# Three stacked blocks on one core: the dilated logarithm folded into a bias table, a mask added in pieces, one PSUM pool, and another order in the last expert

## The chip, the cores and the metric

The kernel runs on one core of a Trainium2 chip. The metric is the device time of one execution in microseconds; smaller is better. Engine names are those of the profile: PE is TensorE (PEld its weight loads), DVE is VectorE, ACT is ScalarE, POOL is GpSimd, SP is SyncE, which here issues nearly all loads.

## What is computed

Three blocks follow each other on x, 256 tokens by 1024 columns, float32.

```python
# first block: Fourier mixing and a gated convolution, then experts that choose their tokens
probs = softmax(h @ w_router + b_router)
vals, idx = top_k(probs.T, cap)                 # 16 experts, 32 tokens each
y = (silu(xe @ w_gate_e) * (xe @ w_up_e)) @ w_down_e * vals
x = rms_norm(x + gate_f * scatter_add(y, idx), g_final)
# second block: one wide projection, two kinds of attention, gates, an output projection
proj = rms_norm_2(x, norm_pre) @ w_in
# third block, two layers: four kinds of attention side by side, then a feed-forward part
o_a = neighborhood_attention(..., rpb)          # rpb as a bias, columns outside a window masked
o_b = diff_attention(..., t5_table[:, :4])      # bias by bucketed distance
o_c = dilated_attention(..., t5_table[:, 4:])   # three patterns (128,1), (512,4), (2048,16), merged
o_d = mla_attention(...)
x = x + concat(o_a, o_b, o_c, o_d) @ w_o
x = x + (silu(h @ w_gate) * (h @ w_up)) @ w_down
```

Three dilated softmaxes merged by their sums are one softmax in which a key counts as often as patterns reach it. The kernel therefore adds the logarithm of that count (-1e30 where it is zero) to the dilated heads' bias. The count depends on the distance of key and query alone.

## The kernel before

Projections of the first, second and third block split each float32 weight piece into a high part (a cast on ACT, L125) and the rest (a subtraction on DVE, L126), and multiply three times on PE: high by high (L173), high input by low weight (L174), low input by high weight (L175). Each projection of 512 columns uses two PSUM banks, one for each half of the tokens. The experts multiply float32 directly, four column groups of the array at a time (gate and up at L851, down at L901).

PSUM has eight banks. The class `Net` opens three pools: `mm` with five banks, `tr` with two (transposes), and `po` with one. Projections, scores, gathers and the experts' sums come from `mm`. The Fourier outputs, one accumulator of the first block's modulation, the router's logits, the experts' up product, and the outputs of all attention heads come from `po`.

The program is written down in one order, and the framework lays it out into the engines' queues: an instruction that is ready earlier by its estimate may go ahead of one that was written first. Each queue is then worked off in order. `tc.issue_after(ins)` queues the instructions of its block behind `ins` where they are on the same engine, with no wait; `N.queued()` does it behind the last matmul noted in `N.last_mm`. Loads are chained in written order (`Net.load`).

In `moe` (the experts) the 16 experts run one after the other: gate and up products, `hs` (L867, L868), transposes to `hT`, then down. The scaled sum `Y` (L903) goes through a matmul with the scatter matrix into four banks `acc` (L907) that stay for all experts. The last expert, whose down weights are packed by columns, makes its two halves of 512 columns one after the other, and calls `out(n)` after each. `out` adds `acc` to x (L813), transposes the new columns and scales and splits them to `hx` (L271, L284, L285), takes squares (L260), and multiplies x by a gain on POOL (L821). During this the first 512-column projection of the second block is begun: `next_load` fetches half of its weights (four k tiles) and splits them in place (`split_to`, two pieces of two k tiles), and `next_products` multiplies them (L173 to L175 with `wr` and `hx`; 24 matmuls a call). The order written is: down half 0, `out(0)`, `next_load`, four k tiles of down half 1, `next_products`, the other twelve, `out(1)` with the second `next_load` in it, `next_products`. The down weights of half 1 come as one load of 2 MB and two of 1 MB, behind the first load of the projection.

In `mixers` (attention of the third block) the four kinds of heads are generators that step once per piece of the running projections: first the latent heads (`latent`, then `heads`), then `differential`, the neighbourhood heads, the dilated heads. A head's scores (L1413) take a bank, `softmax` reads it (L1395 or L1399 on DVE, L1404 on ACT) and scales (L1420), transposes follow (L1426, L1428), then the output product (L1453). `na_bias` loads the neighbourhood bias `nb` and adds the column mask on POOL in one instruction of 128x2048 (L1366). `dil_bias` loads the dilated heads' part `t5b` of the table (L1352) and `c_dil` (L1372), the logarithms for all pairs, and adds them on POOL, four times 128x512 (L1374). The table itself is made once, in `bias_rows` at the end of the first block: eight rows (heads) by 512 distances, from a matmul with a one-hot matrix (L1307), copied to `t5sb` on DVE (L1309), written to memory by POOL's queue (L1310) and broadcast (L1311).

## Time and profile before

| | before |
|---|---|
| median of 3 runs | 2061.4 us (2057.15 to 2067.67) |
| the profiled execution | 2060.89 us, span 2059.1 us |
| PE busy | 1658.0 us (81%) |
| PE weight loads | 997.9 us (48%) |
| DVE busy | 810.1 us (39%) |
| ACT busy | 602.7 us (29%) |
| POOL busy | 171.9 us (8%) |
| moved by DMA | 616.24 MB, mean 299 GB/s |

The page cuts the span into 40 slices of 51.5 us and gives for each engine the busy share in tenths. Matmuls overlap, so PE's busy time says less than its idle time: in the timelines a row's bracket gives the time that the engine stood idle before it, and what ended that. A row whose count is over 1 covers several instructions in a row, from the start of the first to the end of the last. Matmuls of float32 have two records each.

### The profile page before, as it was taken

The numbers are of one execution on the slowest core, as the hardware profiler recorded it, in microseconds if no ns is written. First come the engines' busy times: TensorE is split into PE (matmuls) and PEld (weight loads), VectorE is DVE, ScalarE is ACT, GpSimd is POOL, SyncE is SP. The second block draws the span as 40 slices with busy tenths as digits, with TensorE's granted clock in tenths as the row PEclk, the third lists the DMA queues.
The fourth block names the chain that finished last, engine by engine and source line by source line (L and its number), as shares of the span: only waits on it lengthen the run. The fifth ranks groups of instructions, "written<-read, shape, count | busy, mean of one in ns | idle before, by whom it ended". The sixth has DMA issues, their size and how long they took to land.

```text
span 2059.1 us, 22375 instructions
## 1 busy us (share of the span) xinstructions
PE 1658.0 (81%) x8897; PEld 997.9 (48%) x8897; DVE 810.1 (39%) x1565; ACT 602.7 (29%) x1075; POOL 171.9 (8%) x135
## 2 busy tenths in 40 slices
PE   7999796665655565656555799999999999999998
PEld 4777631111111111111111387777768888768886
DVE  4788610000000000000000357786885555785554
ACT  4455410000000000000000245555554445555443
POOL 1652100000000000000000131102000000110000
PEclk9999898768788888887887999999999999999999
DMA  9988789999999999999999873446335556525552
GB/s 361 378 297 340 319 363 429 429 428 429 430 428 430 429 428 431 429 430 429 429 428 430 332 257 127 143 136 221 117 103 184 184 172 218 170 68 184 184 174 72
DMA packets 128441, 616.24 MB, mean 299 GB/s; under 512 B 8264, under 2 KB 17672, under 8 KB 101328
## 3 DMA queue, kind: packets, MB, share of 16 engines
q1 hardware_dynamic: 124336, 601.46, 74.1%
q0 software_dynamic: 3568, 12.75, 1.9%
q8 instruction: 70, 1.15, 0.2%
q10 hardware_dynamic: 432, 0.60, 0.1%
q14 instruction: 35, 0.29, 0.0%
HBM read 613.72 MB, written 4.24 MB: 300 GB/s over the span
## 4 chain that ended last, share of the span: by engine, by line
PE 47%; DMA 43%; DVE 6%; issue 2%; ACT 1%; SPq 1%; POOL 0%; POOLq 0%; ACTq 0%; DVEq 0%
DMA wr<-we_gate_dram 13%; DMA wr<-we_up_dram 13%; DMA wr<-we_down_dram 13%; PE pb L173 13%; PE pb L174 12%; PE pb L175 12%; DMA wr<-w_in_dram 2%; DVE wl L126 2%; PE pb L271 1%; DMA wr<-w_ada_dram 1%; PE pb L851 1%; PE pb L1413 1%; PE pb L901 1%; ACT sb L1404 1%; PE pb L793 1%
## 5 line engine op out<-in xcount | busy, mean ns | idle before, releaser
L126 DVE TENSOR_TENSOR wl<-wr,wh 128x1024 fp32r<-128x1024 f32 (+1 forms) x380 | 410.2, 1088 | 263.5 <-ACT wh L125 260.0
L851 PE MATMUL pb<-wr,XT 128*32 128x512 f32 x2048 | 319.4, 753 | 214.7 <-DMA wr<-we_up_dram 121.6
L125 ACT CAST wh<-wr 128x1024 fp32r<-128x1024 f32 (+1 forms) x380 | 339.9, 898 | 329.8 <-PE pb L175 302.3
L173 PE MATMUL pb<-wh,hx 128*128 128x512 f32 (+3 forms) x992 | 388.5, 392 | 3.4 <-ACT sb L1404 2.0
L174 PE MATMUL pb<-wl,hx 128*128 128x512 f32 (+3 forms) x992 | 376.6, 380 | 1.7 <-DVE wl L126 1.6
L175 PE MATMUL pb<-wh,hx 128*128 128x512 f32 (+3 forms) x992 | 377.2, 381 | 0.0
L851 PEld LDWEIGHTS pb<-wr,XT 128*32 128x32 f32 x2048 | 61.3, 124 | 454.5 <-DMA wr<-we_up_dram 198.4
L901 PE MATMUL pb<-wr,hT 128*32 128x512 f32 x1024 | 172.7, 803 | 103.0 <-DMA wr<-we_down_dram 96.4
L868 DVE TENSOR_TENSOR hs<-pb,hs 128x512 f32<-128x512 f32 x16 | 11.1, 691 | 554.9 <-PE pb L851 554.9
L173 PEld LDWEIGHTS pb<-wh,hx 128*128 128x128 f32 x992 | 187.2, 189 | 44.0 <-issue 5.8
L174 PEld LDWEIGHTS pb<-wl,hx 128*128 128x128 f32 x992 | 187.7, 189 | 36.5 <-DVE wl L126 4.5
L175 PEld LDWEIGHTS pb<-wh,hx 128*128 128x128 f32 x992 | 187.4, 189 | 35.4 <-issue 0.7
L867 ACT ACTIVATE hs<-pb 128x512 f32<-128x512 f32 x16 | 9.6, 598 | 535.3 <-PE pb L851 534.2
L901 PEld LDWEIGHTS pb<-wr,hT 128*32 128x32 f32 x1024 | 33.9, 129 | 221.0 <-DMA wr<-we_down_dram 143.2
L903 DVE TENSOR_TENSOR Y<-pb,gfr 128x512 f32<-128x512 f32 x15 | 10.4, 692 | 247.1 <-PE pb L901 247.1
L881 ACT COPY Sc<-pb 128x256 f32<-128x256 f32 x16 | 6.0, 373 | 310.3 <-PE pb L879 310.3
L821 POOL TENSOR_TENSOR x<-x,grow 128x512 f32<-128x512 f32 x4 | 5.6, 1420 | 890.5 <-ACT jk L260 890.5
L173 PE MATMUL pb<-wh,ah 128*128 128x512 f32 x176 | 69.9, 397 | 0.0
L174 PE MATMUL pb<-wl,ah 128*128 128x512 f32 x176 | 69.6, 395 | 0.0
L175 PE MATMUL pb<-wh,al 128*128 128x512 f32 x176 | 69.6, 395 | 0.0
L907 PE MATMUL acc<-Y,Sc 64*128 64x512 f32 (+1 forms) x128 | 40.7, 714 | 18.3 <-DVE Y L903 18.3
L404 POOL TENSOR_SCALAR wr<-wr,cs 128x768 f32<-128x768 f32 x14 | 40.3, 2878 | 31.3 <-DMA wr<-w_ada_dram 26.4
(504 smaller groups left out, 1727.4 us busy)
## 6 DMA issues: line engine op xcount, KB each, us to landing
wr<-we_gate_dram SPq DMA_DIRECT2D x64, 2048.0 KB, 38.9
wr<-we_up_dram SPq DMA_DIRECT2D x64, 2048.0 KB, 39.0
wr<-we_down_dram SPq DMA_DIRECT2D x63, 2048.0 KB, 38.9
wr<-w_in_dram SPq DMA_DIRECT2D x62, 1024.0 KB, 8.0
wr<-w_ada_dram SPq DMA_DIRECT2D x24, 1024.0 KB, 12.7
wr<-w_gate_dram SPq DMA_DIRECT2D x22, 1024.0 KB, 5.1
wr<-w_up_dram SPq DMA_DIRECT2D x22, 1024.0 KB, 5.0
wr<-w_down_dram SPq DMA_DIRECT2D x20, 1024.0 KB, 5.0
```

Of the source, the lines that this page charges most:

```text
L125: self.nc.scalar.copy(hi, src)
L126: self.nc.vector.tensor_tensor(lo, src, hi.bitcast(F32), ALU.subtract)
L173: nc.tensor.matmul(o, xh[:, kt, tok], hv[:, k, :], start=kt == first, stop=False)
L174: nc.tensor.matmul(o, xh[:, kt, tok], lv[:, k, :], start=False, stop=False)
L175: self.last_mm = nc.tensor.matmul(o, xl[:, kt, tok], hv[:, k, :], start=False, stop=kt == last).ins
L271: self.nc.tensor.transpose(pv[:, j, h * P:(h + 1) * P], src[:, h, (k + j) * P:(k + j + 1) * P], self.ident)
L404: nc.gpsimd.tensor_scalar(wp, wp, cs[:, k:k + 1], None, ALU.mult)
L793: nc.tensor.matmul(pg, part[:, h, k * P:(k + 1) * P], G[:, h, es].rearrange("p e c -> p (e c)"), start=(h == 0 and i == 0), stop=(h == 1 a ...
L851: N.last_mm = nc.tensor.matmul(pacc[32 * j:32 * j + 32, :], XT[:, k + kk, e, :], wt[:, kk, j * 512:(j + 1) * 512], start=(k + kk == 0), st ...
L901: nc.tensor.matmul(py[32 * q:32 * q + 32, :], hT[:, b, 32 * j:32 * j + 32], wt[:, i, n * 512 - c0:n * 512 - c0 + 512], start=first, stop=l ...
L907: nc.tensor.matmul(acc[n][h], Sc[r, h * P:(h + 1) * P], Y[r, :], start=(e == 0), stop=(e == NE - 1))
L1404: nc.scalar.activation(sb[:, c], (ps if bias is None else sb)[:, c], AF.Exp, bias=mm[:, h:h + 1], accum_out=sm[:, h:h + 1])
```

## The change

- `po` is gone; `mm` has six banks, and all that took a bank from `po` takes one from `mm`.
- Last expert: `next_load` becomes a generator. `out(n)` starts it in both halves, right after the sums into x: the load first, the split queued behind the last of these sums on DVE. The pieces that wait to be multiplied are single k tiles (four a load), and `next_products(n)` multiplies n of them, 6 matmuls each. The order written for half 1 is: eight k tiles of down, two pieces, the other eight k tiles, Y, one piece, L907, the sums into x, one piece, the transposes; the second load's four pieces come last. The down matmuls of half 1 and the pieces are queued on PE in this order.
- `na_bias` adds the mask in eight instructions of 128x256.
- `dil_bias` is gone: `c_dil` is now the logarithm by distance (512 values for the four dilated heads, zeros for the other four), and is added in `bias_rows` when the table is made.

```diff
-        self.mm, self.tr, self.po = ps("mm", 5), ps("tr", 2), ps("po", 1)
+        self.mm, self.tr = ps("mm", 6), ps("tr", 2)
...
             for h in range(2):
                 add = nc.vector.tensor_tensor(x[:, h, cc], acc[n][h], x[:, h, cc], ALU.add).ins
+            ahead = next_load()
+            next(ahead)
+            with tc.issue_after(add):
+                next(ahead, None)
             if n:
-                with tc.issue_after(add):
-                    next_load()
+                next_products(1)
             N.in2.columns(n)
...
         def next_load():
+
             at, raw = next(loads)
             t = N.slot(F32R, wide=True)
-            N.ahead += [(k, p, N.split_to(t[:, 2048 * i:2048 * i + 2048], p)) for i, (k, p) in enumerate(N.pieces(raw, at))]
-
-        def next_products():
+            yield
+            for i, (k, p) in enumerate(N.pieces(raw, at)):
+                hv, lv = N.split_to(t[:, 2048 * i:2048 * i + 2048], p)
+                N.ahead += [(k + j, p[:, j:j + 1], (hv[:, j:j + 1], lv[:, j:j + 1])) for j in range(p.shape[1])]
+
+        def next_products(n=4):
+
             N.ahead_ps = N.ahead_ps or [N.bank(N.mm), N.bank(N.mm)]
-            for k, piece, hl in N.ahead:
-                N.proj_piece(N.ahead_ps, N.in2.hi, N.in2.lo, k, piece, 512, hl=hl)
-            N.ahead = []
+            for k, piece, hl in N.ahead[:n]:
+                with N.queued():
+                    N.proj_piece(N.ahead_ps, N.in2.hi, N.in2.lo, k, piece, 512, hl=hl)
+            del N.ahead[:n]
 
         for e in range(NE):
-            psG, psU = N.bank(N.mm), N.bank(N.po)
+            psG, psU = N.bank(N.mm), N.bank(N.mm)
...
                 c0 = 512 * ns[0]
-                if c0:
-                    next_load()
                 py = N.bank(N.mm)
...
-                        if c0 and at + i == 4:
-                            next_products()
+                        if c0 and at + i == 8:
+                            next_products(2)
...
-                            nc.tensor.matmul(py[32 * q:32 * q + 32, :], hT[:, b, 32 * j:32 * j + 32], wt[:, i, n * 512 - c0:n * 512 - c0 + 512],
-                                             start=first, stop=last, tile_position=(0, 32 * q))
+                            with N.queued() if c0 else nullcontext():
+                                mm = nc.tensor.matmul(py[32 * q:32 * q + 32, :], hT[:, b, 32 * j:32 * j + 32],
+                                                      wt[:, i, n * 512 - c0:n * 512 - c0 + 512],
+                                                      start=first, stop=last, tile_position=(0, 32 * q))
+                            if c0:
+                                N.last_mm = mm.ins
                 nc.vector.tensor_tensor(Y, py, rt.gf if e < NE - 1 else rt.gf_last[:, ns[0], :], ALU.mult)
+                if c0:
+                    next_products(1)
...
-    nc.vector.tensor_copy(sb, pb[:8, :])
+    nc.gpsimd.dma_start(sb, a["c_dil"])
+    nc.vector.tensor_tensor(sb, pb[:8, :], sb, ALU.add)
...
-            nv = nb.rearrange("p h n (r c) -> p (h n r) c", c=64)
-            nc.gpsimd.tensor_tensor(nv, nv, nmask.unsqueeze(1).to_broadcast([P, 32, 64]), ALU.add)
+
+            for h in range(2):
+                for n in range(4):
+                    nv = nb[:, h, n, :].rearrange("p (r c) -> p r c", c=64)
+                    nc.gpsimd.tensor_tensor(nv, nv, nmask.unsqueeze(1).to_broadcast([P, 4, 64]), ALU.add)
             return nb
-
-        def dil_bias():
-            td = t5_bias(4, "t5b")
-            dm = N.m2.tile([P, 2, S], F32, tag="m2", name="dm")
-            nc.gpsimd.dma_start(dm, a["c_dil"].rearrange("p (h k) -> p h k", h=2))
-            for n in range(4):
-                nc.gpsimd.tensor_tensor(td[:, n], td[:, n], dm, ALU.add)
-            return td
...
-        td = dil_bias()
+        td = t5_bias(4, "t5b")
```

## Rows read from the trace of the kernel before

**Rows 1.** The page's forty slices: busy tenths of PE, DVE and the DMAs.
```profile
PE   7999796665655565656555799999999999999998
DVE  4788610000000000000000357786885555785554
DMA  9988789999999999999999873446335556525552
```

**Rows 2.** Busy time by stretch: stretch, length, PE, PEld, DVE, ACT, POOL, clock, DMA, GB/s.
```profile
600.00:1000.00 400.00, 231.64 (x1406) 51.86 (x1406) 18.10 (x35) 6.20 (x13) 0.00 (x0) 0.82 1.01 429
...
1200.00:1250.00 50.00, 49.80 (x389) 40.93 (x388) 25.30 (x54) 26.02 (x41) 3.41 (x3) 1.00 0.54 182
```

**Rows 3.** Timeline, last expert's first half: start, length, engine, line, operation, idle before.
```profile
1151.55 1.92 PE L901 MATMUL pb<-wr,hT 128*32 128x512 f32 x16 [1.19 <-DMA wr<-we_down_dram]
...
1154.38 1.99 ACT L125 CAST wr<-wr 128x1024 fp32r<-128x1024 f32 x2 [8.50 <-DMA wr<-w_in_dram]
1155.46 1.23 DVE L126 TENSOR_TENSOR wr<-wr 128x1024 fp32r<-128x1024 f32 x1 [9.53 <-ACT wr L125]
1156.61 0.68 DVE L903 TENSOR_TENSOR Y<-pb,gfl 128x512 f32<-128x512 f32 x1
...
1157.43 3.45 PE L907 MATMUL acc<-Y,Sc 128*128 128x512 f32 x4 [3.96 <-DVE Y L903]
...
1161.67 0.87 PE L271 MATMUL pb<-ident,x 128*128 128x128 f32 x6 [0.56 <-DVE x L813]
```

**Rows 4.** Timeline of PE, last expert's second half; the first of 24 products, then what follows.
```profile
1163.47 0.50 PE L173 MATMUL pb<-wr,hx 128*128 128x512 f32 x1
...
1169.14 2.78 PE L901 MATMUL pb<-wr,hT 128*32 128x512 f32 x24
...
1172.74 1.98 PE L907 MATMUL acc<-Y,Sc 128*128 128x512 f32 x4 [0.81 <-DVE Y L903]
...
1175.51 0.87 PE L271 MATMUL pb<-ident,x 128*128 128x128 f32 x6 [0.16 <-DVE x L813]
```

**Rows 5.** Timeline of PE: idle time in the Fourier part and in the mixer layers.
```profile
82.14 0.70 PE L520 MATMUL pb<-V,fc 128*128 128x256 f32 x2 [0.61 <-DVE f L126]
...
1449.69 0.70 PE L1413 MATMUL pb<-qkT 96*128 96x256 f32 x2 [1.88 <-ACT sb L1404]
...
1494.55 0.55 PE L1426 MATMUL pb<-ident,sb 128*128 128x128 f32 x3 [0.89 <-DVE sb L1420]
...
1772.60 0.50 PE L173 MATMUL pb<-wh,hx 128*128 128x512 f32 x1 [2.02 <-ACT sb L1404]
...
1776.38 0.70 PE L1413 MATMUL pb<-qkT 96*128 96x256 f32 x2 [1.66 <-ACT sb L1404]
```

**Rows 6.** Timeline of POOL: first layer's dilated adds, second layer's mask.
```profile
1490.55 5.06 POOL L1374 TENSOR_TENSOR t5b<-t5b,dm 128x512 f32<-128x512 f32 x4 [2.42 <-DMA dm<-c_dil_dram]
...
1765.68 4.58 POOL L1366 TENSOR_TENSOR nb<-nb,nmask 128x2048 f32<-128x2048 f32 x1 [4.62 <-issue]
```

**Rows 7.** Timelines of DVE and ACT in the mixer layers.
```profile
1492.10 2.39 DVE L1420 TENSOR_SCALAR sb<-sb,cs 128x256 f32<-128x256 f32 x2
...
1497.54 0.61 DVE L1420 TENSOR_SCALAR sb<-sb,cs 128x256 f32<-128x256 f32 x2
...
1766.23 5.12 DVE L126 TENSOR_TENSOR wl<-wr,wh 128x1024 fp32r<-128x1024 f32 x1
1771.28 0.16 DVE L1401 TENSOR_SCALAR cm<-cm 128x2 f32<-128x2 f32 x1
...
1776.22 0.84 ACT L1474 ACTIVATE rows<-pb,rr 128x256 f32<-128x256 f32 x2
...
1813.68 0.42 DVE L1399 CUSTOM_DVE_ANT_0 sb<-pb,nb 128x256 f32<-128x256 f32 x1
```

**Rows 8.** Busy time by stretch of 1 us, after the first layer's gap (columns as before).
```profile
1451.00:1452.00 1.00, 1.00 (x5) 0.97 (x5) 0.39 (x2) 0.83 (x2) 0.00 (x0) 0.50 0.00 0
```

**Rows 9.** Timeline of POOL at the end of the first block.
```profile
192.05 0.59 POOL L1310 DMA_DIRECT2D t5v<-t5sb  x1 [23.00 <-DVE t5sb L1309]
```

More of the change, by code (lines that the diff above doesn't have):

```diff
@@ L429, in shift_scale @@
         def shift_scale(c):
-            accs, sbs, pt = [N.bank(N.po), N.bank(N.mm)], [], N.bank(N.tr)
+            accs, sbs, pt = [N.bank(N.mm), N.bank(N.mm)], [], N.bank(N.tr)
             def columns(i):
@@ L518, in fourier @@
                     V = Vs[g - 1]
-                    po = N.bank(N.po)
+                    po = N.bank(N.mm)
                     nc.tensor.matmul(po[:, :S], C128, V[:, :S], start=True, stop=False)
@@ L653, in prepare @@
         nc.vector.tensor_tensor(self.w, self.w, self.scf.unsqueeze(2).to_broadcast([P, KT, NE]), ALU.mult)
-        pb = N.bank(N.po)
+        pb = N.bank(N.mm)
         self.pl = pb[:, :2 * NE].rearrange("p (h e) -> p h e", e=NE)
@@ L1191, in st3 @@
                 if s == 0:
-                    self.po = N.po.tile([P, 512], F32, tag="b", name="po")
+                    self.po = N.bank(N.mm, "po")
                     if self.first:
@@ L1448, in st3 @@
                     return
-                po = N.po.tile([P, 512], F32, tag="b", name="po")
+                po = N.bank(N.mm, "po")
                 pts = [pTs.pop(n - 1), pTs.pop(n)]
@@ L1602, in st3 @@
                 if n == 0:
-                    od.append(N.bank(N.po))
+                    od.append(N.bank(N.mm))
                 odv = od[0].rearrange("p (h n d) -> p h n d", h=2, n=4)
@@ L1785, in consts @@
     c["c_t5oh"] = (np.arange(32)[:, None] == bucket[None, :]).astype(np.float32)
-    off = np.arange(S)[None, :] - s[:, None]
-    mult = sum(((off % dil == 0) & (np.abs(off) <= w // 2)).astype(np.int64) for w, dil in ((128, 1), (512, 4), (2048, 16)))
+    mult = sum(((o % dil == 0) & (np.abs(o) <= w // 2)).astype(np.int64) for w, dil in ((128, 1), (512, 4), (2048, 16)))
     lm = np.where(mult > 0, np.log(np.maximum(mult, 1)), -1e30)
-    c["c_dil"] = lm.reshape(2, P, S).transpose(1, 0, 2).reshape(P, 512)
+    c["c_dil"] = np.arange(8)[:, None] // 4 * lm[None, :]
     col = np.arange(64)
```

## The prediction, written before the changed kernel ran

> **What bounds the kernel now.** I read the forty slices first. They show three stages: a first block in which TensorE and the DMAs are both nearly full, the experts, where the DMA digit stays at 9 and TensorE's falls to 5 or 6, and from slice 23 on TensorE at 9 with the DMAs half idle [rows 1]. The table by stretch says the same in numbers: the experts run at 429 GB/s with a DMA share of 1.01, while TensorE has work in 49.80 of 50 us between 1200 and 1250 us [rows 2]. So each stage has its own rule. Inside the experts' stream nothing but bytes counts, and the change moves the same bytes in the same order. Outside it, a saving must be time in which TensorE stood still, or ran at half clock. The timeline of TensorE, filtered for idle time before an instruction, lists all such time, and there is little of it: beside the start, the router and the end of the experts it has the gaps of [rows 5] and a few others that the change doesn't touch. The two places that matter are the last expert and the two mixer layers.
>
> **Part 1, the last expert.** First half of the columns: the last down matmuls start at 1151.55 and issue for 1.92 us, to 1153.47. Y, which scales their sum, starts only at 1156.61, because VectorE's queue holds L126 of the next projection's split ahead of it, and that waits for the cast on ACT, which waits for its weights until 1154.38 [rows 3]. The change queues the two L126 behind the sums into x, so Y can start at 1153.5: 3.1 us earlier. Carried on with the old distances: Y to L907 0.8 us (1154.4), from the first L907 to the end of the transposes 1157.43 to 1162.54, that is 5.1 us (1159.5) [rows 3].
> Second half: before, the 24 products of the next projection stand in one block, 1163.47 to 1169.14, that is 5.7 us or 0.235 us each, ahead of the last 24 records of the down matmuls; these issue for 2.78 us, L907 starts at 1172.74, 0.81 us after them because it waits for Y, and takes 1.98 us, and the transposes end at 1176.38 [rows 4]. After: 16 records of down matmuls (1.92) to 1161.4, 12 products (2.8) to 1164.2, 16 records (1.92) to 1166.1, 6 products (1.4) under Y to 1167.5, L907 (2.0) to 1169.5, 6 products under the sums to 1170.9, transposes (0.87) to 1171.8. That is **4.6 us** earlier than 1176.38.
> What could be late instead: the weights. At 429 GB/s a 2 MB load takes 4.9 us [rows 2], so after 1154.38 the next ones land at about 1159.3 and, in two halves, by 1164.2, just ahead of their use above. This is also the upper bound: even with L907 at 1.98 instead of 3.45 us TensorE would wait for these loads, so the gain ends near 5 us. VectorE: sums end at 1158.5, two L126 of 1.23 us at 1161.0, then the low parts that the first products need at about 1161.9, within their 12. The lower bound: if the products wait for those low parts, the down matmuls queued behind them wait too; one row of that kind, the 3.1 us wait of Y, would take the gain to 1.5, and with a second such wait to -1.5. I take 4.6, because each term is a row. The loads behind, on SP's queue, keep their order and are released by the same instructions, so they come earlier by as much; the second load's split stays between the sums and the transposed columns on VectorE, as before.
>
> **Part 2, six banks in one pool.** Before, five PSUM banks serve the projections (two each) and the scores, and one the head outputs. At 1447.7 and 1770.4 TensorE stops for 1.88 and 2.02 us until ACT's exponential L1404 has read a bank [rows 5]. In the second layer I count the holders: the finished pair of the previous projection, not yet copied out (L1474 at 1776.22 [rows 7]), the new projection's first bank, and two heads' scores: five. No head output is live there, so the sixth bank is free and takes the matmul that waits. The first layer's wait is the same, with the third head's scores as the sixth. A gap of the same kind, 0.61 us in the Fourier part, waits for the single output bank [rows 5].
> After the first layer's gap the clock stands at 0.50, so 1.2 GHz, through three whole stretches of 1 us like the one shown [rows 8] and part of a fourth, which costs some 1.7 us; the rows of the second layer's two gaps show matmuls of the usual length behind them. So the first layer holds 1.88 to 3.6 us.
>
> **Part 3, the mask in pieces.** POOL adds the mask in one instruction; the second layer's takes 4.58 us, from 1765.68 to 1770.26 [rows 6]. VectorE's L126 of 128x1024, 1.23 us when alone [rows 3], took 5.12 us beside it, 3.9 more, and ended at 1771.35, about one such instruction after POOL did [rows 7]. The softmax steps of the latent heads stand behind it on VectorE (L1401 at 1771.28 [rows 7]), and the second layer's gaps of 2.02 and 1.66 us wait for their exponentials [rows 5]. Eight pieces cost POOL more: from 4.58 us for 2048 columns and 5.06/4 = 1.27 for 512 [rows 6] a piece of 256 is about 0.71 us, eight 5.7, 1.1 us more per layer. The first head that reads the bias does so at 1813.68 [rows 7], 43 us later, so that is hidden.
> Beside the four 1.27 us adds of the dilated bias VectorE's pair L1420 took 2.39 us, against 0.61 a little later [rows 6, 7]: it was done more than a microsecond before the four adds were, so it got in between two. So a piece delays a VectorE instruction by up to one piece, 0.7 us. The page SBUF — State Buffer of the Trainium skill (section "SBUF: two separate sides") calls the ports that the two engines share an exclusive lock for the whole instruction, and by it every such VectorE instruction, not only the first, may wait for a piece. The trace agrees as far as one instruction goes: L126's 5.12 us end behind POOL's 4.58 [rows 6, 7]. That is a rival below, priced from the rows.
> Parts 2 and 3 aim at the same gaps, so they are summed once: first layer 1.88 to 3.6, second 3.7. I take **2.8 and 3.0**, most of it, since a chain that is delayed less may still be late once.
>
> **Part 4, the dilated logarithm.** The four adds per layer (5.06 us of POOL) and a load go. They lie beside the pair L1420 that lost 1.78 us, and TensorE waits 0.89 us for it [rows 5 to 7]; the second layer repeats the pattern. **1.8 us** (0 to 3.6). The new work is one small load and an add in place of a copy in the first block. POOL sat idle for 23.0 us before its next transfer there, waiting for the sum that the new add will make [rows 9], which covers the load. If the load came late, that transfer and, far ahead of its readers, the table's broadcast would slip by microseconds: cost nothing.
>
> **The sum.** 4.6 + 2.8 + 3.0 + 1.8 + 0.3 (half of the Fourier gap) = 12.5 us. Against it stands what no row shows: with another pool every instruction order after it is laid out anew, and single new waits of the size of [rows 5] (0.6 to 2.0 us) can appear; the bound is two gained or four lost, +4 to -8, and I take -1.5. So 11 us. The profiled execution took 2060.9 us, its span 2059.1 and 1.8 around it; it gives 2049.9. The median of the runs is 0.5 higher, so I say 2050.5 us, 0.5% less; 0.5% (10.3 us) is also about what a measurement of this kernel can tell from no change.
>
> **Rivals.**
> A. Only the last expert gains. In the mixers the gaps close, but the heads' chain on VectorE, whose digits are 6 to 8 in these slices [rows 1], sets the pace and TensorE waits a little later. For it: all mixer gaps name ACT or VectorE. Against: two of them are waits for a bank, not for data. 2061 - 5 = 2056 us. Chance 0.2.
> B. The pieces only cut the same blocking up. In the second layer four VectorE instructions (L126, L1401, two L1420) would wait 0.7 us each, 2.8 instead of the 3.9 of [rows 7]; the sixth bank still removes 2.02, the other 1.66 stays: 1.7 us less than forecast, 2052 us. The page named above is the rule behind it. Chance 0.1.
> C. Slower. The head outputs and the long-lived output of the differential heads now take banks from the pool of scores and projections. With two output projections' four banks held, only two are left for a pair of scores and an output. Each time the output must wait for a score's exponential, TensorE stands 2 us and may lose 1.7 us of clock [rows 5, 8]: 3.6 us. There are two outputs in each of three head groups and two layers, 12, and 8 in the second block. It decides from the fourth wait on (15 us against 12.5); with ten it is 2061 + 25 = 2086 us. Against it: before, five and one hold the same load, and a shared pool can always hand out at least as many. Chance 0.08.
> D. The change doesn't do what it says: the queueing edge orders L126 behind the sums, but the laid-out order puts the first 12 products ahead of data, so that Y and the second half come as late as before. Then only the mixers gain, 2061 - 6 = 2055 us. Chance 0.07.
>
> **How the numbers follow.** The forecast has 0.55, spread over 2044 to 2055 by its bounds. Eight in ten of all cases lie between 2043 and 2060: the forecast, A, B and D whole; above lies C, below the case in which all bounds fall well. Below 2051.1 (faster by over 0.5% of the median, 2061.4) lie some 0.7 of the forecast, 0.4 of B and the better ends of A and D: 0.46. Slower by over 0.5% is most of C: 0.07. The rest, 0.47, is within.
>
> **What would show it.** Y of the first half some 0.1 us after the last down matmul, with both L126 behind the sums; transposes of the second half ending near 1172; no 1.88 and 2.02 us gaps before L1413 and L173 in the latent heads; L126 near 1.2 to 2 us beside the mask; no POOL adds on the dilated bias and L1420 at 0.3 us each. The forecast is wrong if TensorE's idle time in the mixers keeps its sum, or if the time between the experts' last load and the second block's first own projection does not shrink by 4 us.

## The result, and the profile after

The changed kernel took 2042.2 us (median of 4 runs, 2041.7 to 2043.4) against 2062.5 us for the kernel before, a ratio of 0.9905 with a 95% interval of 0.9882 to 0.9928. That is some 20 us less, where the forecast said 11. The profiled execution took 2041.8 us with a span of 2040.0, so 19.1 us less than the span of before.

Busy time of the two mixer layers (columns as in [rows 2]), before and then after:

```profile
1404.00:1539.00 135.00, 129.49 (x680) 99.85 (x679) 101.57 (x285) 71.89 (x166) 20.43 (x20) 0.99 0.46 149
1723.00:1856.00 133.00, 126.22 (x670) 97.16 (x669) 100.09 (x277) 70.19 (x163) 20.10 (x20) 1.00 0.47 151
```
```profile
1404.00:1533.00 129.00, 125.63 (x674) 96.26 (x673) 98.02 (x282) 73.66 (x172) 13.55 (x17) 1.00 0.46 151
1723.00:1849.00 126.00, 124.04 (x668) 95.35 (x667) 96.99 (x279) 71.80 (x168) 12.77 (x17) 1.00 0.47 153
```

These stretches hold the surprise. The same work took 135.00 and 133.00 us before, and 129.00 and 126.00 after. Of the 13.0 us that these layers lost, 6.0 had been marked as TensorE's busy time, and only some 1.7 of that was at half clock [rows 8].

Timeline of after in the last expert (start, length, engine, line, operation, idle before), against [rows 3, 4]:

```profile
1148.73 3.56 PE L909 MATMUL pb<-wr,hT 128*32 128x512 f32 x16 [2.06 <-DMA wr<-we_down_dram]
...
1152.34 0.69 DVE L914 TENSOR_TENSOR Y<-pb,gfl 128x512 f32<-128x512 f32 x1 [7.69 <-PE pb L909]
1153.18 1.96 PE L920 MATMUL acc<-Y,Sc 128*128 128x512 f32 x4 [0.89 <-DVE Y L914]
...
1155.78 2.35 DVE L126 TENSOR_TENSOR wr<-wr 128x1024 fp32r<-128x1024 f32 x2
...
1168.01 1.04 PE L271 MATMUL pb<-ident,x 128*128 128x128 f32 x8
```

The last down matmul of the first half ends at 1152.29 and Y starts 0.05 us later, with both L126 behind the sums. The second half's transposes end at 1169.05. Before, they ended at 1176.38 [rows 4], 7.3 us later, of which 2.8 are the earlier start of this stage (1148.73 against 1151.55).

Timeline of POOL in after: the end of the first block, and the mask of the second layer; then VectorE's instructions beside that mask:

```profile
178.74 0.58 POOL L1322 DMA_DIRECT2D t5sb<-c_dil_dram  x1 [18.57 <-DVE gate L554]
179.36 2.37 POOL L404 TENSOR_SCALAR wr<-wr,cs 128x768 f32<-128x768 f32 x1
181.81 2.16 POOL L405 TENSOR_TENSOR adas<-wr,adas 128x768 f32<-128x768 f32 x1
...
1747.95 2.81 POOL L1383 TENSOR_TENSOR nb<-nb,nmask 128x256 f32<-128x256 f32 x4 [0.61 <-DMA nb<-rpbd]
1751.52 3.01 POOL L1383 TENSOR_TENSOR nb<-nb,nmask 128x256 f32<-128x256 f32 x4
```

```profile
1750.25 1.60 DVE L126 TENSOR_TENSOR wl<-wr,wh 128x1024 fp32r<-128x1024 f32 x1 [3.16 <-ACT wh L125]
...
1754.24 1.37 DVE L126 TENSOR_TENSOR wl<-wr,wh 128x1024 fp32r<-128x1024 f32 x1
1755.54 0.15 DVE L1410 TENSOR_SCALAR cm<-cm 128x2 f32<-128x2 f32 x1
```

L126 takes 1.60 and 1.37 us where it meets the pieces, against 5.12 in [rows 7]. A load that waits 18.57 us stands ahead of L404 and L405 in POOL's queue. Before, there was no such load [rows 9], and these two ran earlier (POOL, before):

```profile
164.77 2.36 POOL L404 TENSOR_SCALAR wr<-wr,cs 128x768 f32<-128x768 f32 x1 [3.54 <-DMA wr<-w_ada_dram]
167.21 1.84 POOL L405 TENSOR_TENSOR adas<-wr,adas 128x768 f32<-128x768 f32 x1
```

TensorE's idle time in after (timeline of PE). The first two rows are new; the other two are all that is left of the 1.88, 2.02 and 1.66 us in [rows 5]:

```profile
1350.57 0.43 PE L1154 MATMUL po<-pT,mv 128*64 128x256 f32 x1 [0.34 <-DVE pT L1141]
...
1352.78 0.65 PE L1154 MATMUL po<-pT,mv 128*64 128x256 f32 x2 [0.77 <-DVE pT L1141]
...
1442.94 0.33 PE L271 MATMUL pb<-ident,rows 128*128 128x128 f32 x1 [0.87 <-ACT rows L1483]
...
1761.00 0.33 PE L271 MATMUL pb<-ident,rows 128*128 128x128 f32 x1 [0.18 <-ACT rows L1483]
```

**Where the time went.** Because idle rows say so little about this, I compared stages: the same two TensorE instructions mark a stage's ends in every kernel, and the table gives how much longer (+) or shorter (-) the stage is than in the first profile of before, in us. The marks are at these times of before: load's place 144.92 to 186.05, last expert 1151.55 to 1210.02, end of block 2 1348.02 to 1393.97, latent heads 1439.94 to 1457.97 and 1769.97 to 1780.10, dilated stage 1490.06 to 1503.02 and 1814.95 to 1828.08, output projection 1512.94 to 1529.91 and 1838.01 to 1861.92.

```
kernel               load's  last   block 2  latent      dilated     output proj.
                     place   expert end      1st   2nd   1st   2nd   1st   2nd
after                -1.07   -5.15  +1.17   -2.58 -3.73 -1.96 -1.93 -1.40 -1.38
after_again          -1.09   -4.10  +1.23   -2.31 -3.85 -1.95 -1.94 -1.37 -1.35
before_again         +0.14   +0.95  +0.02   -1.66 -1.80 +0.06 +0.20 +0.02 +0.03
pool_alone           +0.18   +0.49  +1.21   +3.23 +1.65 +0.14 +0.04 -1.39 -1.37
fold_alone           -1.08   +0.69  +0.02   +0.76 -2.36 -1.95 -1.95 +0.02 +0.03
mask_alone           +0.06   +0.83  +0.04   -2.19 -3.93  0.00 +0.03 +0.02  0.00
last_alone           +0.14   -5.52  +0.02   +1.15 -2.37 +0.04 +0.14 +0.02 +0.02
before_queue_hold    -1.09   +0.50  +0.01   +1.99 -2.37 +0.20 +0.04  0.00 +0.01
before_dil_one_input +0.14   +0.92   0.00   -1.66 -2.37 -1.60 -1.64  0.00 +0.01
after_5and1          -1.09   -5.50  +0.04   -2.10 -3.91 -1.94 -1.94 +0.02 +0.01
after_mask_whole     -1.08   -3.92  +1.17   +3.16 -0.62 -1.97 -1.95 -1.40 -1.39
after_no_mask        -1.09   -5.17  +1.22   -3.45 -3.85 -1.95 -1.95 -1.40 -1.38
after_held_bank      -1.09   -5.23  +0.02   -2.37 -3.86 -1.96 -1.94 -1.40 -1.37
after_held_16        -1.09   -3.86  +0.02   -2.56 -2.42 -1.95 -1.97 -1.39 -1.37
after_no_edge        -1.09   -1.61  +1.19   -2.25 -3.91 -1.96 -1.93 -1.41 -1.38
after_one_block      -1.09   -3.42  +1.23   -2.13 -3.75 -1.96 -1.97 -1.37 -1.37
after_pieces_late    -1.09   -5.14  +1.21   -2.39 -3.85 -1.95 -1.94 -1.37 -1.36
after_timed          -1.09   -5.11  +1.17   -2.49 -3.85 -1.96 -1.95 -1.37 -1.40
held_timed           -1.09   -5.65  +0.04   -2.11 -3.87 -1.94 -1.97 -1.40 -1.38
```

Six of the nine columns take one of two values, with or without one part of the change (before_dil_one_input alone lies between). The last expert and the latent heads scatter from execution to execution: the six profiles with five banks and one and a whole mask have -1.66 to +1.99 us in the first latent stage and -2.37 to 0.00 in the second, where the first profile of before, the measure of this table, is the longest. The stages of after sum to 18.0 us. The other 1.1 of its 19.1 us lie in the rest of the first block and in the experts' stream, which differ by as much between two executions of one kernel (below). The shares: last expert 5.2, the mask in pieces 6.3 (2.6 and 3.7), the folded logarithm 5.0 (1.1 and twice 1.95), the pool 1.6 (2.8 less 1.2).

### The profile page after: what moved, and what is told of

It reads as the page before. It is cut to its first block, busy times and chain, and to the rows that moved or that the text cites. A ratio compares the mean times of both kernels' runs of the same rounds, so it can differ in the third digit from the quotient of the medians.

```text
span 2040.0 us, 22389 instructions
## 1 busy us (share of the span) xinstructions
PE 1641.4 (80%) x8897; PEld 993.7 (49%) x8897; DVE 802.7 (39%) x1565; ACT 600.8 (29%) x1075; POOL 162.6 (8%) x140
## 4 chain that ended last, share of the span: by engine, by line
PE 48%; DMA 43%; DVE 5%; issue 1%; ACT 1%; SPq 1%; POOL 0%; POOLq 0%; ACTq 0%; DVEq 0%
DMA wr<-we_down_dram 15%; DMA wr<-we_gate_dram 14%; DMA wr<-we_up_dram 13%; PE pb L173 13%; PE pb L174 13%; PE pb L175 13%; DVE wl L126 2%; PE pb L271 1%; SPq L75 1%; PE pb L909 1%; PE pb L860 1%; DMA wr<-w_ada_dram 1%; PE pb L1422 1%; ACT sb L1413 1%; PE pb L1435 1%
## 5 line engine op out<-in xcount | busy, mean ns | idle before, releaser
L126 DVE TENSOR_TENSOR wl<-wr,wh 128x1024 fp32r<-128x1024 f32 (+1 forms) x380 | 406.9, 1080 | 260.7 <-ACT wh L125 257.3
L909 PE MATMUL pb<-wr,hT 128*32 128x512 f32 x1024 | 164.1, 767 | 107.5 <-DMA wr<-we_down_dram 99.3
L920 PE MATMUL acc<-Y,Sc 64*128 64x512 f32 (+1 forms) x128 | 39.0, 700 | 14.4 <-DVE Y L914 14.4
L404 POOL TENSOR_SCALAR wr<-wr,cs 128x768 f32<-128x768 f32 x14 | 38.9, 2781 | 28.7 <-DMA wr<-w_ada_dram 23.3
```

Of the source, the lines that this page charges most:

```text
L126: self.nc.vector.tensor_tensor(lo, src, hi.bitcast(F32), ALU.subtract)
L404: nc.gpsimd.tensor_scalar(wp, wp, cs[:, k:k + 1], None, ALU.mult)
L909: mm = nc.tensor.matmul(py[32 * q:32 * q + 32, :], hT[:, b, 32 * j:32 * j + 32], wt[:, i, n * 512 - c0:n * 512 - c0 + 512], start=first, s ...
L920: nc.tensor.matmul(acc[n][h], Sc[r, h * P:(h + 1) * P], Y[r, :], start=(e == 0), stop=(e == NE - 1))
```

## The experiments

Times are medians, ratios are to the kernel before on the same chip, with 95% intervals.

**One part alone.** Each is the kernel before with one group of the change's lines.

pool_alone:
```
-self.mm, self.tr, self.po = ps("mm", 5), ps("tr", 2), ps("po", 1)
+self.mm, self.tr = ps("mm", 6), ps("tr", 2)      (and N.bank(N.mm) for every N.po)
```


> The kernel before with one edit: the five banks and the one become a single pool of six; the mask, the dilated bias and the last expert stay as before. Theory 1 (the bank is behind every gain that the forecast had not counted in places where a matmul takes a new bank): the Fourier part starts its later products about 0.6 us earlier, the 1.88 and 2.02 us gaps of the two layers go, and the output-projection stages gain 1.4 us each as they did in the full change: in all 6 to 8 us faster, ratio about 0.9965, less what the end of the second block gives back. Theory 2 (the bank only closes the marked gaps; the output-projection stages gain from POOL's missing adds): 3 to 5 us, ratio about 0.998, and the stage from the transposes of orow to fn_r takes the 32.85 us of before.

Measured: 2062.2 us, 1.0008 (0.9998 to 1.0017). Both theories fall as sums. The output-projection stages do gain 1.4 us each, but in the profiled execution the latent heads lose 3.2 and 1.7. That execution took 2065.3 us, one of four at 2065 to 2067, where the other seven took 2059 to 2062; so the size of this loss is that of the longer ones. At the median, too, the gain of 2.8 less 1.2 us is gone. The timeline shows why (POOL, VectorE, TensorE):

```profile
1444.26 5.08 POOL L1366 TENSOR_TENSOR nb<-nb,nmask 128x2048 f32<-128x2048 f32 x1 [5.58 <-DMA nb<-rpbd]
...
1444.82 4.55 DVE L1401 TENSOR_SCALAR cm<-cm 128x2 f32<-128x2 f32 x1
...
1450.54 1.13 PE L1413 MATMUL pb<-qkT 96*128 96x256 f32 x4 [1.14 <-ACT sb L1404]
...
1454.68 0.48 PE L271 MATMUL pb<-ident,rows 128*128 128x128 f32 x1 [3.00 <-ACT rows L1474]
```

L1401 handles two columns and takes 0.16 us when alone [rows 7]. Here it takes 4.55, until POOL's mask has ended; the exponential L1404 waits for it, and TensorE for that. The sixth bank does not take this wait away: it comes in front of later instructions.

fold_alone:
```
+nc.gpsimd.dma_start(sb, a["c_dil"])
-nc.vector.tensor_copy(sb, pb[:8, :])
+nc.vector.tensor_tensor(sb, pb[:8, :], sb, ALU.add)
-    nc.gpsimd.tensor_tensor(td[:, n], td[:, n], dm, ALU.add)      (four per layer, and the load of dm)
```


> The kernel before with one edit: the dilated logarithm is added to the eight-row table in the first block, the four POOL adds per layer and their load go. Theory 1: the dilated stages gain about 2 us each (forecast: 0.9 each), and the first block about 1.3 us, because the load of the small table stands in POOL's queue ahead of the last adds of the conditioning, which then no longer run beside VectorE at 165 to 170 us: in all 5 to 6 us, ratio about 0.9973. Theory 2 (the forecast's): 0.9 us per layer and nothing in the first block: 1.8 us, ratio 0.999, r_r on POOL at 245.4 as before.

Measured: 2054.5 us, 0.9967 (0.9954 to 0.9979). Theory 1 holds in each stage: 1.95 us in each dilated stage and 1.08 in the first block. L1421 (the old L1420) takes 0.61 us where [rows 7] had 2.39:

```profile
1492.40 0.61 DVE L1421 TENSOR_SCALAR sb<-sb,cs 128x256 f32<-128x256 f32 x2
```

mask_alone: the eight pieces of the change's diff, nothing else.


> The kernel before with one edit: the mask is added in eight pieces instead of one instruction. Theory 1 (the mask's long hold of VectorE costs one of the two gaps, the bank the other): 1.5 to 2 us faster, the 1.66 us gap of the second layer goes, the 2.02 stays. Theory 2 (the pieces only cut the same blocking up): within 0.5 us of before, both gaps stay. Theory 3 (the bank was the whole wait): as theory 2, but with VectorE's L126 at 1.2 to 2 us beside the pieces.

Measured: 2056.5 us, 0.9976 (0.9966 to 0.9986). More than any of the three: both gaps of the second layer go with five banks and one, so the forecast's pairing of one gap with the bank was wrong.

last_alone: the new order of the last expert, nothing else.


> The kernel before with one edit: the last expert's new order. Theory 1: the last expert gains 5 us, as in the full change, and the end of the second block gives nothing back, because the new 0.3, 0.8 and 0.65 us gaps there come from the common pool: 5 us, ratio 0.9976, in_r 5 us earlier. Theory 2 (the gaps there come with the earlier start, since weights or the normalising chain are then late): in_r only about 3.3 us earlier and the whole 3.3 us, ratio 0.9984.

Measured: 2054.5 us, 0.9970 (0.9960 to 0.9981). The stage gains 5.5 us and the end of the second block gives nothing back (+0.02). Theory 1.

**One part undone, in the changed kernel.**

after_5and1: the pools of before again.


> The changed kernel with the pool undone: five banks and one again, all else as changed. Theory 1 (the six-bank pool pays in the full change): its two output-projection stages lose 1.4 us each (before and changed: 18 and 16.6 us from the transposes of orow to the end of the dilated heads), the end of the second block wins back about 1.2, so some 1.5 to 3 us slower than the changed kernel, ratio to before about 0.992; the latent stages stay as short as in the changed kernel, because the pieces of the mask and not the bank closed their gaps. Theory 2 (the forecast's: the sixth bank takes the matmul that waits): the 1.88 and 2.02 us gaps come back, and it is 5 to 7 us slower, ratio 0.9935 or above.

Measured: 2044.8 us, 0.9924 (0.9911 to 0.9936); theory 1. Latent heads as short as with six banks (-2.10, -3.91), output projections as before. TensorE's timeline in the first layer's output-projection stage says what the sixth bank does there; first after, then after_5and1:

```profile
1504.71 0.70 PE L1422 MATMUL pb<-dl 64*128 64x256 f32 x4
...
1508.06 1.11 PE L1462 MATMUL po<-pT,dl 128*64 128x256 f32 x8
```
```profile
1503.57 1.13 PE L1422 MATMUL pb<-dl 64*128 64x256 f32 x4
...
1506.59 0.65 PE L1462 MATMUL po<-pT,dl 128*64 128x256 f32 x2
...
1508.65 1.08 PE L1462 MATMUL po<-pT,dl 128*64 128x256 f32 x6
```

TensorE has no idle time in either, and yet the same matmuls take 16.99 us with a bank less and 15.58 with six. The kernel writes the scores of two heads (L1422) in turn, each on half of the array's rows. With six banks they are issued in turn and run two at a time: four records in 0.70 us. With five and one, four records of one head are issued alone and follow each other, in 1.13 us, and the other head's come later. Likewise the output products of two heads (L1462, half of the array's columns each): two of them go alone. Over the stage L1422 is busy for 1.4 us against 2.3, and L1462 for 2.8 against 3.4; the rest agrees within 0.1 us. So the gain is neither a wait nor faster work, but matmuls that run side by side.

after_mask_whole: the mask in one instruction again.


> The changed kernel with the mask added in one instruction again, all else as changed. Theory 1 (POOL's one instruction holds VectorE and with it the latent heads; the bank alone only moves the wait, as it did alone): the latent stages lose what the pieces alone gained plus what the pool alone lost, about 5 us in each layer, so 8 to 11 us slower than the changed kernel, ratio to before 0.995, with idle TensorE of some 4 us beside the mask in each layer. Theory 2 (the parts only add up): 6 us slower, ratio 0.9935. Theory 3 (the sixth bank closes the gaps by itself): under 1.5 us slower.

Measured: 2049.1 us, 0.9950 (0.9938 to 0.9963); theory 1 by its ratio. The profiled execution is one of two at 2052 us (the other three took 2048 to 2049), with 5.7 us in the first layer's stage and 3.1 in the second's; the median is 7 us above the changed kernel's, between theories 2 and 1. The rows of the first layer (POOL, VectorE, TensorE, and busy time by stretch as in [rows 8]):

```profile
1436.81 4.59 POOL L1380 TENSOR_TENSOR nb<-nb,nmask 128x2048 f32<-128x2048 f32 x1 [4.51 <-DMA nb<-rpbd]
```
```profile
1437.20 5.27 DVE L126 TENSOR_TENSOR wl<-wr,wh 128x1024 fp32r<-128x1024 f32 x1
1442.40 0.15 DVE L1407 TENSOR_SCALAR cm<-cm 128x2 f32<-128x2 f32 x1
```
```profile
1443.73 1.13 PE L1419 MATMUL pb<-qkT 96*128 96x256 f32 x4 [0.81 <-ACT sb L1410]
...
1447.87 0.48 PE L271 MATMUL pb<-ident,rows 128*128 128x128 f32 x1 [3.01 <-ACT rows L1480]
```
```profile
1448.00:1449.00 1.00, 1.00 (x6) 0.93 (x7) 1.00 (x4) 1.00 (x2) 0.00 (x0) 0.50 0.00 0
```

The idle time is 3.8 us, and from 1447, near its end, to 1453 the clock stands at 0.50 (1.2 GHz). The pool is that of the changed kernel. So the pieces closed the gaps, and with the whole mask a sixth bank is no help: where the mask began 1.2 or 1.3 us after the stage's first mark, the stage took 18.79 us with five and one (fold_alone) and 21.19 with six (here), and where it began 2.4 or 2.3 us after it, 19.18 (last_alone) and 21.25 (pool_alone).

after_no_mask: the eight additions left out.


> The changed kernel without the additions of the mask to the neighbourhood bias (left out: the mask's columns are not barred, the rest is computed). It measures what the eight pieces still cost. Theory 1 (a piece delays VectorE by at most its own 0.7 us, and the chain absorbs it): within 1 us of the changed kernel, ratio 0.990. Theory 2 (the pieces cut the same blocking up, rival B): 3 to 5 us faster than the changed kernel, ratio 0.988, with VectorE's instructions in the latent stages shorter by as much.

Measured: 2041.3 us, 0.9906 (0.9893 to 0.9920). The pieces still cost 0.9 us in the first layer and 0.1 in the second. Theory 1; rival B falls.

after_no_edge:
```
-            with tc.issue_after(add):
-                next(ahead, None)
+            next(ahead, None)
```


> The changed kernel without the queueing edge that puts the next projection's split behind the sums into x (the split is then issued when it is ready; one L126 comes ahead of the first half's Y again, nothing changes on TensorE). Theory 1 (the forecast's: the edge takes 3.1 us of wait off Y): Y starts some 2 to 3 us later and the kernel is 2 to 3 us slower than the changed one. Theory 2 (in the new order TensorE has other products to do meanwhile, and only the second half's place counts): under 1 us slower.

Measured: 2046.0 us, 0.9931 (0.9918 to 0.9943); 3.5 us of the stage are gone against the first profile of after, 2.5 against the second; the second is in theory 1's range. Only VectorE's order differs, and TensorE stands still for it:

```profile
1152.51 1.23 DVE L126 TENSOR_TENSOR wr<-wr 128x1024 fp32r<-128x1024 f32 x1 [8.25 <-DMA wr<-we_down_dram]
```
```profile
1153.66 0.68 DVE L913 TENSOR_TENSOR Y<-pb,gfl 128x512 f32<-128x512 f32 x1
```
```profile
1154.49 3.75 PE L919 MATMUL acc<-Y,Sc 128*128 128x512 f32 x4 [3.06 <-DVE Y L913]
```

The wait is the forecast's own chain. The four L919 take 3.75 us instead of the 1.96 of after, but that is not the edge's: they do so in after_again too, with the edge and a short wait:

```profile
1151.01 3.75 PE L920 MATMUL acc<-Y,Sc 128*128 128x512 f32 x4 [0.88 <-DVE Y L914]
```

In all three executions the clock stood at 0.50 during the down matmuls before Y, behind 2.1 to 2.3 us of waiting for weights. In after it was back at 1.00 when L920 began; in the other two it was still 0.50.

after_one_block:
```
-    next_products(2)                 (ahead of the last eight down matmuls)
+    next_products()
-    next_products(1)                 (under Y, and under the sums)
```


> The changed kernel with the last expert's 24 products of the first load in one block again, ahead of the second half's last eight down matmuls and of Y (the edge stays). Theory 1 (the forecast's: products under Y, and under the sums, hide 0.8 us of wait for Y and 1 to 2 us of wait for the sums): the second half's transposes end about 2 us later, and the kernel is 1.5 to 2.5 us slower than the changed one. Theory 2 (the products only change places, TensorE does the same work): within 0.5 us.

Measured: 2044.9 us, 0.9924 (0.9910 to 0.9937); 1.7 us of the stage against the first profile of after. That column alone is not far from scatter (with the new order whole the stage lies between -3.86 and -5.65); the medians, over 2 us apart, and the wait for Y, which has no idle time in after at this place and is back here, speak for theory 1:

```profile
1168.29 1.98 PE L916 MATMUL acc<-Y,Sc 128*128 128x512 f32 x4 [0.81 <-DVE Y L912]
```

**The disputed waits.**

before_queue_hold: the kernel before with
```
+    nc.gpsimd.dma_start(sb, a["c_t5oh"][:8, :])
```


> The kernel before, with one small load more in POOL's queue in the first block: eight rows of the one-hot table into the buffer of the small table's sum, which the copy then overwrites; the result does not depend on it, and the four POOL adds per layer stay. Theory 1 (the fold's gain in the first block is the load's place in POOL's queue, ahead of the last multiply and add of the conditioning, which leave VectorE alone at 165 to 170 us): TensorE is 1.1 us earlier from 186 us on, measured against its own lead at 145 us, VectorE's L126 there takes 0.7 instead of 2.14 us, and the dilated stages stay as before: 1 us faster, ratio 0.9995. Theory 2 (the gain comes from the addition in place of the copy, or from the smaller constant): no change in the first block.

Measured: 2058.2 us, 0.9986 (0.9977 to 0.9995). The stage is 1.09 us shorter and the dilated stages are as before: theory 1. The same stretch of POOL and VectorE, first before_again (where the load is missing), then this kernel:

```profile
166.05 2.20 POOL L405 TENSOR_TENSOR adas<-wr,adas 128x768 f32<-128x768 f32 x1
```
```profile
166.47 3.13 DVE L403 SCALAR_TENSOR_TENSOR adas<-wr,cs,adas 128x1280 f32<-128x1280 f32 x1
```
```profile
178.66 0.59 POOL L1309 DMA_DIRECT2D t5sb<-c_t5oh_dram  x1 [18.55 <-DVE gate L554]
179.28 2.36 POOL L404 TENSOR_SCALAR wr<-wr,cs 128x768 f32<-128x768 f32 x1
181.72 2.17 POOL L405 TENSOR_TENSOR adas<-wr,adas 128x768 f32<-128x768 f32 x1
```
```profile
166.94 1.54 DVE L403 SCALAR_TENSOR_TENSOR adas<-wr,cs,adas 128x1280 f32<-128x1280 f32 x1
```

L403 takes 3.13 us beside L405, and 1.54 where L405 is held back in the queue. In the first profile of before it was an L126 that stood there, with 2.14 us instead of 0.7.

before_dil_one_input:
```
-    nc.gpsimd.tensor_tensor(td[:, n], td[:, n], dm, ALU.add)
+    nc.gpsimd.tensor_scalar(td[:, n], td[:, n], dm[:, 0, 0:1], None, ALU.add)
```


> The kernel before with the four POOL additions of the dilated bias made with one tensor input (a column of the loaded table is added as a scalar for each partition; the dilated logarithm is then wrong, the amount of data written is the same). Theory 1 (VectorE is held by POOL instructions with two tensor inputs only, as the trace shows it beside L404 and L405 in the first block): VectorE's pair L1420 takes 0.6 us instead of 2.39 beside them, the dilated stage gains 2 us in each layer as with the fold, 4 us in all, ratio 0.998. Theory 2 (any POOL instruction holds VectorE, or the load and buffer count): L1420 stays at 2 us or more, the stages as before, or longer if these additions are longer.

Measured: 2056.4 us, 0.9980 (0.9971 to 0.9989). POOL works longer, 6.24 us against 5.06 [rows 6], and holds VectorE less:

```profile
1492.19 6.24 POOL L1374 TENSOR_SCALAR t5b<-t5b,dm 128x512 f32<-128x512 f32 x4 [2.64 <-DMA dm<-c_dil_dram]
```
```profile
1493.52 1.09 DVE L1420 TENSOR_SCALAR sb<-sb,cs 128x256 f32<-128x256 f32 x2
```

The stages gain 1.60 and 1.64 of the fold's 1.95 us. So most of the fold's worth there is the second tensor input of POOL's additions; the load of dm, which stayed, was not the cost. Theory 1, though L1420 at 1.09 us is not quite at its 0.6.

after_held_bank:
```
-    self.po = N.bank(N.mm, "po")
+    held[:] = held or [N.bank(N.mm, "po")]
+    self.po = held[0]
```


> The changed kernel with one edit: in the second block the output of the head pairs keeps one bank of the six for the whole block, as it had one before, so that the matmuls on pT of a new pair are again issued behind the reading of the old output; the pool stays six everywhere else. Theory 1 (the pool gives 1.4 us in each output-projection stage and takes 1.25 us at the end of the second block, both by the order of TensorE's instructions): 1.2 us faster than the changed kernel, about 2041.0 us, no gaps of 0.34 and 0.77 us before L1154, the output-projection stages as in the changed kernel. Theory 2 (the loss comes from the earlier start of the second block or from the weights' loads): the gaps stay and the time is the changed kernel's.

Measured: 2042.1 us, 0.9912 (0.9899 to 0.9926). In the trace theory 1 holds: the 0.34 and 0.77 us gaps are gone and the end of the second block is as before (+0.02). The time does not show it. Both kernels on one chip:


> The changed kernel with one bank held for the second block's outputs, timed on the same chip. Theory 1 (the 1.3 us of the trace lie on TensorE's path and stay won to the end): 1.3 us below the changed kernel, 2040.7 us. Theory 2 (what is won there is lost again behind it, or in the experts' scatter): within 0.4 us of it.

Measured: 2041.8 us against 2042.5 for after_timed, 0.9908 (0.9891 to 0.9924) and 0.9910 (0.9895 to 0.9925). A gain of 1.2 us can't be told from none here.

**Open ends.** A second profile of each kernel:


> The kernel before once more, for a second profile. Theory 1 (the first block's 1.3 us beyond the load's effect is the scatter of one execution, from the weights' arrival): the first block's end differs by 0.5 to 1.5 us from the first profile of before, while the stages of the mixers agree within 0.1 us, except the latent stages, where the mask's start against the heads is decided by the moment the loads land. Theory 2 (the kernel's own): the first block ends at 245.4 and the 2.02 us gap stands again.

> The changed kernel once more, for a second profile. Theory 1: the first block's end moves by 0.5 to 1.5 us against the first profile of the changed kernel, all stages behind the experts agree within 0.1 us, the latent stages too, because the pieces end before the heads wait for VectorE. Theory 2: all agree, the first block too.

Measured: 2057.5 and 2042.0 us. The kernel before differs from itself by 1.7 and 1.8 us in the latent stages; the changed one by 0.3 and 0.1. TensorE's two gaps of the second layer in before_again, against 2.02 and 1.66 in [rows 5]:

```profile
1769.07 0.50 PE L173 MATMUL pb<-wh,hx 128*128 128x512 f32 x1 [0.22 <-ACT sb L1404]
...
1772.85 0.70 PE L1413 MATMUL pb<-qkT 96*128 96x256 f32 x2 [1.66 <-ACT sb L1404]
```

So the 2.02 us gap belonged to one execution: with a whole mask it depends on where among the heads' steps the mask begins (4.3 us before the stage's first mark in before, 7.8 in before_again). In the first layer the mask stands the same in both, and so does the gap of 1.88 us. What differs is the clock behind it, 0.50 in [rows 8] and 1.00 in before_again:

```profile
1451.00:1452.00 1.00, 1.00 (x6) 0.83 (x5) 0.94 (x3) 0.54 (x2) 0.00 (x0) 1.00 0.00 0
```

Against before_again the pieces gain 0.9 and 1.9 us, not 2.6 and 3.7. The rest of the first block's gain is of this kind too (last section).

after_pieces_late (the pieces in reverse order) and after_held_16 (a held bank, and pieces of 128 columns):


> The changed kernel with the eight pieces in reverse order, so that the first piece waits for the last load of the table as the whole mask did. Theory 1 (the cutting counts: VectorE gets in between two pieces): the latent stages are at most 0.7 us longer than in the changed kernel. Theory 2 (the early start counts): 2 to 4 us longer in a layer, as with the whole mask.

> The changed kernel with one bank held for the second block's outputs and the mask in sixteen pieces of 128 columns. Theory 1 (what the pieces still cost, 0.9 us in the first layer against no mask, is the length of a piece): 0.4 us shorter in the first layer's latent stage, and 1.3 us at the end of the second block from the held bank: 2040.5 us. Theory 2 (a start of its own for each piece costs POOL time that comes back on VectorE): the latent stages as with eight pieces or longer, 2041 us.

Measured: 2042.0 us, 0.9910 (0.9896 to 0.9923), and 2043.1 us, 0.9913 (0.9899 to 0.9926). The first tells nothing: its first four pieces still begin at 1429.51, so the early start wasn't taken away. For the first layer the traces of after and before_again answer in its stead: the pieces end 1.6 us later than the whole mask did (1438.80 against 1443.06, on a stage 5.9 us earlier), and the stage is 0.9 us shorter, so there the cutting counts. In the second layer the pieces also begin earlier against the stage (10.0 us before its first mark, the whole mask of before_again 7.8), because four of them need only the first loads of the bias; what the early start is worth there is not shown. In after_held_16 sixteen pieces take 8.7 us of POOL in the second layer against 5.8 for eight, and the stage is 1.4 us longer; theory 2. No complete kernel here is faster than the changed one beyond the scatter.

## Why the prediction was wrong

**The premise.** "Outside it, a saving must be time in which TensorE stood still, or ran at half clock." Of the mixers' 13.0 us, 6.0 came out of TensorE's busy time, and half clock was only 1.7 of them; 2.8 came from two heads' matmuls that run side by side, and some 1.4 from the dilated stages. The list of idle time before an instruction did not show what another order of the same matmuls frees, nor the full delay of a chain that TensorE follows. This is the step that failed; it put the output-projection stages (2.8 us) and the load's place (1.1 us) at nothing, and made part 4 too small by 2.1.

**Part 1, 4.6 us: right.** 5.2 in the first profile after, 4.1 in the second, 5.5 alone. Y, the split's place and the transposes came as named, and each half of the mechanism showed a price: 2.5 to 3.5 us for the edge, and over 2 us at the median for the split products.

**Parts 2 and 3, 5.8 us: the sum near, the cause wrong.** 6.3 us came, from the pieces alone, but that the sum came near is luck: the second profile of before has 3.5 us less in these stages, and measured from it only 2.8 came. I had read "waits for the exponential L1404" as a wait for a bank, and counted holders to prove it. L1404 itself waited for L1401, which stood behind the L126 that POOL held [rows 6, 7]; one step further along the chain would have said so. I had both rows, 4.58 us of mask and 5.12 of L126, and gave them half of the gap. The 1.7 us of half clock behind the first layer's gap, too, were those of one execution.

**Part 4, 1.8 us: mis-sized and incomplete.** 3.9 us in the dilated stages. I took the 0.89 us that TensorE was marked idle, and passed over a second wait for L1420 in the same stage (TensorE, before), which was not among the gaps that the change does not touch:

```profile
1498.03 0.30 PE L1426 MATMUL pb<-ident,sb 128*128 128x128 f32 x1 [0.36 <-DVE sb L1420]
```

But the whole gain is larger than both; what VectorE had lost was 1.78 us on L1420 and 0.34 on the L1401 behind it (0.49 in the trace of before, against 0.15 alone), and 1.95 of these 2.12 came through, as they would where VectorE's chain sets the pace. And the new load "costs nothing" was true and missed the point: standing in POOL's queue it moved two instructions away from VectorE, for 1.1 us.

**The Fourier gap, 0.3 us.** It is closed, but TensorE then waits 2.5 to 3.0 us for the conditioning's rows at 132 us in any case; there after_5and1, which has the gap, and after_mask_whole, which has not, stand equal (at 132.75 us). Nothing.

**The deduction, 1.5 us.** The new order did cost 1.2 us, at the end of the second block, and the same pool gave 2.8 in the output projections. With one bank for outputs a pair's matmuls on pT had to wait until the last output was read, and projection matmuls went ahead of them; with six they were issued at once and waited for pT.

**Together.** 11 us, plus 2.1 (part 4 in the mixers), 1.1 (the load's place), 2.8 (output projections), 0.5 (parts 2 and 3), 0.6 (part 1), less 0.3 (Fourier), plus 0.3 (the deduction), is 18.1; the trace has 19.1 and the medians 20. These terms are differences to one profile of before; the span of before_again is only 15.7 us above that of after, so a us or two of the sum is the choice of the execution. The range ended at 2043.0 because its bounds were drawn around the listed gaps.

**The rivals.** A and D did not come true. B: without any mask the stages are only 0.9 and 0.1 us shorter. The rule that I quoted beside it, from the page SBUF — State Buffer of the Trainium skill (section "SBUF: two separate sides"), that the shared ports are locked for a whole instruction, agrees with L1401's 4.55 us for two columns; that an addition with one tensor input holds VectorE far less (1.09 against 2.39 us) was not in what I had taken from it. C, outputs that wait, came only as the 1.2 us above.

## What to carry to other kernels

Compare the length of stages between fixed instructions, and find what each engine's chain loses beside other work; a list of idle gaps is a lower bound. Follow a wait at least one releaser further than the row names, above all where POOL has a long instruction with two tensor inputs on. A transfer put into a queue is also a wait for all that stands behind it, which can be a gain or a loss.

## What the runs showed of the hardware

The same wait of TensorE was followed by different clocks in different executions: the 1.88 us of the first latent stage by 0.50 in before and 1.00 in before_again. In the first block it waits for the conditioning's rows, 3.01 us in before and 2.98 in before_again, 2.52 in after and 2.97 in after_again. Busy time by stretch, before and then before_again:

```profile
132.00:136.00 4.00, 3.56 (x10) 1.75 (x11) 2.03 (x5) 0.00 (x0) 3.92 (x3) 0.63 0.48 147
```
```profile
132.00:136.00 4.00, 3.53 (x13) 2.22 (x14) 2.98 (x5) 0.00 (x0) 3.92 (x3) 0.78 0.49 143
```

The granted clock is 0.63 in the one and 0.78 in the other, in the next 4 us 0.52 and 0.79, and the stretch from the end of the wait to the matmul at 144.92 us of before is 1.6 us shorter in the second. The two profiles of after differ in it by the same 1.6 us, so it is no part of the change: over all twenty profiles it takes 10.9 us (seven) or 12.2 to 12.5 (thirteen), in both kernels, and waits of 2.5 and of 3.0 us stand before either.

Two heads' scores, each on half of the array's rows, took 0.70 us for four records issued in turn, and 1.13 us for four records of one head.

A VectorE instruction on two columns took 4.55 us beside a POOL addition with two tensor inputs, and a pair on 256 columns 1.09 us beside additions with one, where it had 2.39 beside additions with two and 0.61 beside none. In the first block of before an L126 of 128x512 took 0.69 us beside L404, which has one tensor input, and another 2.14 us beside L405, which has two.
